# First stage of a hybrid decoder step: transposes, copies and sums in another order

## The chip, the cores and the metric

The kernel runs on one core of one Trainium2 chip. The metric is the device time of one execution in microseconds (us). Engines are called as in the profile: PE is TensorE (PEld its weight loads), DVE is VectorE, ACT is ScalarE, POOL is GpSimd, SP is SyncE, which issues most DMAs.

## What is computed

One decoder layer for a prompt of 1024 tokens and eight single sample tokens, width 1024, all in float32:

```
xn = rmsnorm(h, pre_g)
u, v, z_a, x_b, z_b, g_a, g_b = split(xn @ w_in)          # 1024 -> 7 x 1024
vn = layernorm(gelu(v))
y_a = gelu(u) * chunk_spatial_mix(vn, w_s, b_s) * silu(z_a)
y_b = pool_branch(x_b) * silu(z_b)
m = sigmoid(g_a) * (y_a @ w_pa) + sigmoid(g_b) * (y_b @ w_pb)
h = h + rmsnorm(m @ w_out, post_g)
e = p @ w_ple                                              # p: 256 wide
h = h + rmsnorm(sigmoid(rmsnorm(h, ple_in_g) @ w_pg) * e, ple_out_g)
```

The change touches only what stands at the program's start: the product `e = p @ w_ple`, the first rmsnorm (its squares, roots and scalings of x), and the transposes of x and p.

## The kernel before, in words

Float32 operands are cut in two parts: a high part rounded to TensorE's fp32r by ACT, and a low part, the rest, by DVE (`split`, L352). A product is then three matmuls: high by high, high by low, low by high. The large products use Strassen's seven products on quarters of the operand (`strassen`, L649); the quarters of x are named B11, B12, B21, B22, and sums of them T1 to T4.

All operations are recorded by a planner (L301 is the line that plays them, so nearly every row of the profile names L301; tiles tell them apart). What `begin` (L1743) records is fixed: on each engine it runs in the order in which it is written. What follows is ordered by the planner's costs and due times. Each engine works through its own queue in order, so an instruction that waits holds up all behind it.

`begin` does the following, in the order written:

- DMAs of p (`p_load`), of the two halves of w_ple (`we.fetch`), of x's eight row tiles (`x_load`) and of the first weights (vraw).
- `we.high` and `we.low` (L802, L809) cut w_ple, tile by tile: wehi on ACT, welo on DVE. `p_turn` (L1682) transposes p on PE into a tile pp and cuts it into ph (ACT) and pl (DVE). `embed_terms` (L1700) are the matmuls of e; `embed_out` (L1718) copies a finished e out of PSUM and stores it.
- `norm_root(t)` (L853): ACT squares the row tile t of x and sums it, DVE adds epsilon, POOL raises to the power -0.5. `norm_scale(t)` (L857): DVE scales x's tile in place by that root.
- `x_half(j, kp)` (L872): PE transposes two column blocks (kp) of four row tiles of x (j is 0 for tiles 0 to 3 and 1 for tiles 4 to 7) into a PSUM tile pst, eight 128x128 transposes; ACT and DVE cut pst into high and low. For j = 1 and kp below 2 the cut is left to later sums. `x_out` (L900) copies pst to the buffer `big` (ACT), and `x_whole` (L906) instead writes high plus low of an already cut quarter to `big`, on POOL.
- `x_extra` (L911): eight small transposes of the sample's rows into the tile pxe, which four multiplications by the gain on DVE copy to `big`. `steps[0]` to `steps[3]` are the first Strassen products of v; their `evacuate` copies the accumulator acc out of PSUM on ACT.

PSUM is held in two pools: three regions of two banks, and two single banks. The single banks serve in turn p's pp, w's gain vectors, the first two pst, the accumulators of `steps[0]` to `steps[3]`, pxe and pp again. A tile that takes a bank waits until the tile that held it has been read.

The stretch around the second half of x stands in `begin` as `steps[3].run()`, `x_extra()`, `steps[3].evacuate()`, `p_turn(1, 0)`, `x_half(1, 2)`, `p_turn(1, 1)`, `x_half(1, 3)`, `x_tail()`, `embed(4)`.

Of the kernel before, what the change touches and what calls it, by code (L numbers as in the profile page):

```python
# [13 lines left out]
ALU = mybir.AluOpType  # L14

P = 128
D = 1024
# [4 lines left out]
HALF = 512  # L22
# [285 lines left out]
def hybrid_step(  # L308
# [7 lines left out]
    nc = tc.nc  # L316
# [15 lines left out]
    def slot(name, shape=(P, T), dt=F32):  # L332
        n_name[0] += 1
        return plan.tile(spool.tile(list(shape), dt, tag="slot", name=f"{name}_{n_name[0]}", bufs=SLOTS,
                                    padded_shape=None), "slot")
# [38 lines left out]
    nc = plan  # L374
# [15 lines left out]
    def root(part, n=P, r=None):  # L390

        t, r = sm("ms"), sm("rstd") if r is None else r
        nc.vector.tensor_scalar(out=t[:n], in0=part[:n], scalar1=EPS, scalar2=None, op0=ALU.add)
        nc.gpsimd.tensor_tensor(out=r[:n], in0=t[:n], in1=mhalf[:n], op=ALU.pow)
        return r

    def square_sum(src, n=P, bias=0.0, scratch=None):

        s = sm("ssq")
        out = junk[:n, : src.shape[1]] if scratch is None else scratch[:n]  # L400
        nc.scalar.activation(out=out, in_=src, func=AF.Square, scale=D ** -0.5, bias=bias, accum_out=s[:n])
        return s
# [15 lines left out]
    def quarter(kp, j):  # L418
        both = big[:, 2 * kp : 2 * kp + 2, :].rearrange("p a t -> p (a t)")
        return (both[:, 2 * HALF :] if j else both[:, : 2 * HALF]).rearrange("p (k t) -> p k t", k=2)  # L420
# [431 lines left out]

    def norm_root(t):  # L853
        xt, n = (xe, NS) if t == S else (xts[t], P)
        roots[t] = root(square_sum(xt[:n], n, scratch=slot("squares", (P, D))), n)

    def norm_scale(t):  # L857
        xt, n = (xe, NS) if t == S else (xts[t], P)
# [11 lines left out]
    col = lambda i, k: gvec[:, i * NB + k : i * NB + k + 1]  # L870

    def x_half(j, kp):  # L872

        if kp == 0:
            ps = [bank("pst") for _ in range(2)]
        else:
            ps = region("pst")
            ps = [ps[:, kk] for kk in range(2)]
        for kk in range(2):
            k = 2 * kp + kk  # L880
            for i in range(4):
                nc.tensor.transpose(ps[kk][:, i * P : (i + 1) * P], xts[4 * j + i][:, k * P : (k + 1) * P], ident)
        if j and kp < 2:
            turned[j, kp] = ps
            return
        hi, lo = x_parts(j, kp)
        for kk in range(2):
            nc.scalar.activation(out=hi[:, kk, :HALF], in_=ps[kk], func=AF.Copy, scale=col(0, 2 * kp + kk))
        for kk in range(2):
            nc.vector.scalar_tensor_tensor(out=lo[:, kk, :HALF], in0=ps[kk], scalar=col(0, 2 * kp + kk),  # L890
                                           in1=f32(hi[:, kk, :HALF]), op0=ALU.mult, op1=ALU.subtract)
        turned[j, kp] = ps

    turned = {}

    def x_parts(j, kp):
        what = f"B{kp // 2 + 1}{j + 1}"
        return xop.parts[what, kp % 2] if (what, kp % 2) in xop.parts else xop.new(what, kp % 2)
# [7 lines left out]
    def x_whole(j, kp):  # L906

        hi, lo = (f32(x[:, :, :HALF]) for x in xop.parts[f"B{kp // 2 + 1}{j + 1}", kp % 2])
        nc.gpsimd.tensor_tensor(out=quarter(kp, j)[:, :, :HALF], in0=hi, in1=lo, op=ALU.add)

    def x_extra():  # L911
        ps = bank("pxe").rearrange("p (k t) -> p k t", k=NB)
# [6 lines left out]
    def x_tail():  # L919
        for kp in range(2, NB // 2):  # L920
            split(quarter(kp, 1)[:, :, HALF:], *(x[:, :, HALF:] for x in x_parts(1, kp)))
# [760 lines left out]
    def p_turn(h, q, ks=range(2), by=None):  # L1682
        hi, lo = pcut[h]
        ps = bank("pp").rearrange("p (k c) -> p k c", k=2)
        for k in ks:
            for t in range(2):
                nc.tensor.transpose(ps[:, k, t * P : (t + 1) * P], praw[h][:, 2 * q + t, k * P : (k + 1) * P], ident)
        ks, c = slice(ks[0], ks[-1] + 1), slice(2 * q * P, (2 * q + 2) * P)
        if by is None:
            split(ps[:, ks], hi[:, ks, c], lo[:, ks, c])  # L1690
        else:
            by.tensor_copy(out=hi[:, ks, c], in_=ps[:, ks])
            sub(lo[:, ks, c], ps[:, ks], f32(hi[:, ks, c]))
# [6 lines left out]
    def embed_terms(t, n, terms):  # L1700

        if t == 2:
            e_ps[t, n] = e_ps.get((t, n)) or bank("e")
        elif t not in e_ps:
            e_ps[t] = region("e")
        out = e_ps[t, n] if t == 2 else e_ps[t][:, n]
        todo = left.setdefault((t, n), 6)
        for k, (i, j) in terms:
            nc.tensor.matmul(out, pcut[t // 4][i][:, k, t % 4 * P : (t % 4 + 1) * P], we.at(n, k)[j],
                             start=todo == 6, stop=todo == 1)  # L1710
            todo -= 1
        left[t, n] = todo
# [30 lines left out]
    def begin():  # L1743
        psl = slot("psamp", (P, PLE))
        p_load(0, 0)
        for i, v in enumerate((pre_g, pool_scale, ple_in_g)):
            dma(vecs[i * NB : (i + 1) * NB, :], v[0].rearrange("(k p) -> k p", p=P), nc.scalar)
        we.fetch(0)
        we.fetch(1)
        p_load(0, 1)  # L1750
        for t in range(4):
            x_load(t)
        dma(xe[:NS], x_sample)
        steps[0].loads()
        steps[1].loads()
        for t in range(4, NB):
            x_load(t)
        for q in range(2):
            p_load(1, q)
        dma(psl[:NS], p_sample)  # L1760
        praw.append(psl)
        fetched[0] = 6
        early_loads()

        def busy(n):
            ps = region("warm")[:, 0]
            for _ in range(n):
                nc.tensor.matmul(ps, junk[:, :P], junk, start=True, stop=True)

        p_new(0)  # L1770
        busy(5)
        we.high(0, 0)
        p_turn(0, 0, (0,), nc.vector)
        busy(1)
        p_turn(0, 0, (1,))
        we.high(0, 1)
        for k in range(2):
            we.low(0, k)
        for k in range(2):
            for i in (HH, LH):  # L1780
                for t in range(2):
                    embed_terms(t, 0, [(k, i)])
        for t in range(2):
            embed_terms(t, 0, [(0, HL), (1, HL)])
        for k in range(2):
            we.high(1, k)
        for k in range(2):
            we.low(1, k)
        vps = bank("vecs")
        nc.tensor.transpose(vps[:, : 3 * NB], vecs[: 3 * NB, :], ident[: 3 * NB, : 3 * NB])  # L1790
        nc.vector.tensor_copy(gvec, vps[:, : 3 * NB])
        embed_terms(0, 1, [(0, HH), (0, LH), (1, HH), (1, LH)])
        p_turn(0, 1)
        embed_terms(0, 1, [(0, HL), (1, HL)])
        embed_terms(1, 1, [(0, HH), (0, LH), (1, HH), (1, LH), (0, HL), (1, HL)])
        norm_root(0)
        norm_root(1)
        norm_scale(0)
        embed(2)
        norm_root(2)  # L1800
        embed_out(0, nc.vector)
        norm_root(3)
        norm_scale(1)
        norm_scale(2)
        embed_out(1)
        embed(3)
        norm_scale(3)
        embed_out(2)
        vweights[0].prepare("A11")
        embed_out(3, nc.vector)  # L1810
        for kp in range(3):
            x_half(0, kp)
        vweights[1].prepare("A11")
        x_half(0, 3)
        steps[0].run()
        vweights[0].prepare("A12")
        vweights[1].prepare("A12")
        norm_root(4)
        steps[0].evacuate()
        steps[1].run()  # L1820
        norm_root(S)
        norm_root(5)
        steps[1].evacuate()
        norm_scale(4)
        norm_root(6)
        norm_scale(S)
        norm_root(7)
        for t in range(5, NB):
            norm_scale(t)
        x_whole(0, 0)  # L1830
        x_whole(0, 1)
        steps[2].run()
        steps[2].evacuate()
        x_out(0, 3)
        x_out(0, 2)
        steps[3].run()
        for t in (8, 4, 5):
            steps[t].loads()
        steps[8].loads = None
        x_extra()  # L1840
        steps[3].evacuate()
        p_new(1)
        p_turn(1, 0)
        x_half(1, 2)
        p_turn(1, 1)
        x_half(1, 3)
        x_tail()
        embed(4)
        x_out(1, 2)
        x_half(1, 0)  # L1850
        x_out(1, 0)
        embed_out(4, nc.vector)
        x_out(1, 3)
        x_half(1, 1)
        x_out(1, 1)
        vweights[0].add_up()
        xop.combine("T3")
        embed(5)
        embed_out(5)
        prepared[0] = 4  # L1860
# [52 lines left out]
```

## Time and profile before

| | |
|---|---|
| median of 3 runs | 979.65 us (979.62 to 981.12) |
| the profiled execution's own time | 980.18 us |
| its span, first to last instruction | 978.4 us |
| PE busy | 964.9 us (99%) |
| DVE busy | 799.1 us (82%) |
| ACT busy | 532.3 us (54%) |
| POOL busy | 73.2 us (7%) |
| mean granted PE clock | 0.996 of full speed |

A row of the timeline gives the start, the time it took (merged rows: from the first one's start to the last one's end), engine, line, operation, the tile written and the tiles read with partitions x elements, the count, and in brackets the idle time of the engine before it with what ended it. Rows that follow each other on PE overlap by some 0.15 to 0.25 us, since a matmul's start lies before the end of the one ahead; pace is read from start to start. A row of the windows view gives for each stretch the sum and the time each engine was busy in it, the clock that was granted to PE, the share of the DMA engines and the GB/s.

### The profile page before, as it was taken

The numbers are of one execution on the slowest core, as the hardware profiler recorded it, in microseconds if no ns is written. First come the engines' busy times: TensorE is split into PE (matmuls) and PEld (weight loads), VectorE is DVE, ScalarE is ACT, GpSimd is POOL, SyncE is SP. The second block draws the span as 40 slices with busy tenths as digits, with TensorE's granted clock in tenths as the row PEclk, the third lists the DMA queues.
The fourth block names the chain that finished last, engine by engine and source line by source line (L and its number), as shares of the span: only waits on it lengthen the run. The fifth ranks groups of instructions, "written<-read, shape, count | busy, mean of one in ns | idle before, by whom it ended". The sixth has DMA issues, their size and how long they took to land. (4 is left out here: it accounts for less than half of the span.)

```text
span 978.4 us, 16078 instructions
## 1 busy us (share of the span) xinstructions
PE 964.9 (99%) x6077; PEld 860.4 (88%) x6077; DVE 799.1 (82%) x1263; ACT 532.3 (54%) x899; POOL 73.2 (7%) x143
## 2 busy tenths in 40 slices
PE   9999999999999999999999999999999999999996
PEld 6789999999999999999999999999999986888775
DVE  6796658887789698979897987697799799769786
ACT  6775998865444433344543333552363273967662
POOL 1400000000000000001000100000000001312222
PEclk9999999999999999999999999999999999999999
DMA  9445572422483253656735167884583393799966
GB/s 334 160 151 129 135 171 87 167 94 78 141 298 130 95 187 118 242 196 221 258 131 173 37 228 249 273 312 151 176 302 107 126 349 97 169 280 363 292 183 194
DMA packets 119308, 185.56 MB, mean 190 GB/s; under 512 B 29183, under 2 KB 75735, under 8 KB 119222
## 3 DMA queue, kind: packets, MB, share of 16 engines
q1 hardware_dynamic: 117102, 177.11, 53.8%
q0 software_dynamic: 2080, 7.41, 4.3%
q8 instruction: 48, 0.79, 0.3%
q14 instruction: 30, 0.25, 0.1%
q10 hardware_dynamic: 48, 0.01, 0.0%
HBM read 125.85 MB, written 53.87 MB: 184 GB/s over the span
## 5 line engine op out<-in xcount | busy, mean ns | idle before, releaser
L301 DVE TENSOR_TENSOR u<-acc,u 128x520 f32<-128x520 f32 (+1 forms) x84 | 58.3, 695 | 23.8 <-PE acc L301 21.9
L301 POOL TENSOR_TENSOR rstd<-ms,mhalf 128x1 f32<-128x1 f32 (+1 forms) x36 | 29.7, 825 | 230.1 <-DVE ms L301 208.7
L301 POOL MEMSET u<- 128x8 f32 x32 | 3.3, 104 | 491.3 <-PE acc L301 232.2
L301 ACT ACTIVATE u<-acc 128x512 f32<-128x512 f32 x36 | 21.4, 594 | 23.7 <-PE acc L301 23.1
L301 ACT ACTIVATE paw<-pas 128x512 fp32r<-128x512 f32 x16 | 10.1, 628 | 30.7 <-DVE pas L301 25.5
L301 ACT ACTIVATE pbw<-pbs 128x512 fp32r<-128x512 f32 x16 | 10.0, 629 | 29.3 <-DVE pbs L301 26.1
L301 DVE TENSOR_TENSOR v<-acc,v 128x520 f32<-128x520 f32 (+1 forms) x20 | 13.9, 693 | 12.8 <-PE acc L301 12.6
L301 ACT ACT_TABLE_LOAD x17 | 21.8, 1283 | 4.3 <-PE acc L301 1.8
L301 DVE TENSOR_TENSOR big<-big 128x1024 f32<-128x1024 f32 (+4 forms) x20 | 23.7, 1217 | 0.0
L301 ACT ACTIVATE big<-v 128x1024 uint16<-128x1024 uint16 x16 | 18.6, 1170 | 7.2 <-DMA v<-vw 7.2
L301 PE MATMUL accm<-qh,wpoolw 128*128 128x260 f32 (+1 forms) x96 | 20.9, 320 | 0.0
L301 ACT ACTIVATE zbw<-zbs 128x512 fp32r<-128x512 f32 x16 | 10.0, 628 | 16.5 <-DVE zbs L301 10.2
L301 ACT ACTIVATE gbw<-gbs 128x512 fp32r<-128x512 f32 x16 | 10.0, 624 | 15.7 <-DVE gbs L301 13.7
L301 DVE TENSOR_TENSOR big<-mix,big 128x256 f32<-128x256 f32 x32 | 12.7, 419 | 6.9 <-ACT big L301 6.8
L301 ACT ACTIVATE big<-mix 128x256 f32<-128x256 f32 x32 | 11.7, 379 | 12.4 <-PE mix L301 12.0
L301 DVE TENSOR_TENSOR acc<-acc,u 128x512 f32<-128x512 f32 (+1 forms) x16 | 11.2, 699 | 8.8 <-PE acc L301 8.8
L301 ACT ACTIVATE uw<-us 128x512 fp32r<-128x512 f32 x16 | 10.0, 626 | 14.0 <-DVE us L301 6.8
L301 ACT ACTIVATE vw<-v 128x1024 uint16<-128x1024 uint16 x16 | 16.2, 1045 | 2.3 <-DVE v L301 2.3
L301 PEld LDWEIGHTS accm<-qh,wpoolw 128*128 128x128 f32 x96 | 15.6, 188 | 1.9
L301 ACT ACTIVATE u<-u 128x1032 f32<-128x1032 f32 (+1 forms) x8 | 6.8, 853 | 18.9 <-DVE u L301 18.8
L301 ACT ACTIVATE gb<-gb 128x1032 f32<-128x1032 f32 (+1 forms) x8 | 6.8, 854 | 18.5 <-DVE gb L301 18.5
L301 ACT ACTIVATE zaw<-zas 128x512 fp32r<-128x512 f32 x16 | 10.1, 629 | 12.4 <-PE acc L301 5.2
(666 smaller groups left out, 3599.7 us busy)
## 6 DMA issues: line engine op xcount, KB each, us to landing
ga<-ga SPq DMA_DIRECT2D x16, 516.0 KB
gb<-gb SPq DMA_DIRECT2D x16, 516.0 KB
vraw<-in_w_in_dram SPq DMA_DIRECT2D x22, 256.0 KB
ya<-za SPq DMA_DIRECT2D x8, 516.0 KB
yb<-zb SPq DMA_DIRECT2D x8, 516.0 KB
x<-in_x_prompt_dram SPq DMA_DIRECT2D x8, 512.0 KB
e<-e SPq DMA_DIRECT2D x8, 512.0 KB
garaw<-in_w_in_dram SPq DMA_DIRECT2D x8, 512.0 KB
```

The lines of the kernel that those rows point to most:

```text
L301: getattr(getattr(self.nc, e), method)(*args, **kwargs)
```

## The change

Six edits, all in `begin` and its helpers:

1. `we.low` of w_ple's first tile moves ahead of the second tile's `we.high`, and the matmuls with the first tile's low part ahead of those with the second tile's high part.
2. Among the first row tiles of x, the square of tile 0 moves on ACT ahead of the copy of p's second pp; `embed_out(0)` moves up on DVE, ahead of the scaling of tile 0.
3. The square of x's tile 5 is made by DVE (`square_here`, L404) instead of ACT.
4. The sums `x_whole` are made by DVE instead of POOL, and later: the first after `x_extra`, the second after `x_tail`.
5. `x_half` is split in `x_turn` (transposes) and `x_cut`; for the second half of x, the eight transposes of kp 2 stand ahead of p's first transposes, those of kp 3 ahead of p's second. `steps[3].evacuate()` stands ahead of `x_extra()`.
6. The copy of `embed_out(4)` goes from DVE to ACT and stands ahead of `x_out(1, 0)`.

On PE near the start, one piece of the difference; e_134 and e_135 are e's accumulators of row tiles 0 and 1, wehi_129 and welo_130 hold both tiles of w_ple's first column half, ph and pl are p's parts:

```order
 L301 MATMUL e_134<-wehi_129,pl_127 128x512
 L301 MATMUL e_135<-wehi_129,pl_127 128x512
+L301 MATMUL e_134<-welo_130,ph_126 128x512
+L301 MATMUL e_135<-welo_130,ph_126 128x512
 L301 MATMUL e_134<-wehi_129,ph_126 128x512
 L301 MATMUL e_135<-wehi_129,ph_126 128x512
 L301 MATMUL e_134<-wehi_129,pl_127 128x512
 L301 MATMUL e_135<-wehi_129,pl_127 128x512
-L301 MATMUL e_134<-welo_130,ph_126 128x512 x2
-L301 MATMUL e_135<-welo_130,ph_126 128x512 x2
+L301 MATMUL e_134<-welo_130,ph_126 128x512
+L301 MATMUL e_135<-welo_130,ph_126 128x512
```

Two of the four low-part matmuls now stand ahead of the first matmul that reads the second tile's high part.

On PE after the last product ahead of x's second half, before; p_124 is p's second half, x_89 to x_92 are x's tiles 4 to 7:

```order
L301 MATMUL acc_186<-xB21h_176,vw_180 128x512
L301 MATMUL pxe_207<-ident,xe_84 128x8 x8
L301 MATMUL pp_210<-ident,p_124 128x128 x4
L301 MATMUL pst_211<-ident,x_89 128x128
L301 MATMUL pst_211<-ident,x_90 128x128
L301 MATMUL pst_211<-ident,x_91 128x128
```

and in the change:

```order
L301 MATMUL pxe_207<-ident,xe_84 128x8 x8
L301 MATMUL pst_208<-ident,x_89 128x128
L301 MATMUL pst_208<-ident,x_90 128x128
L301 MATMUL pst_208<-ident,x_91 128x128
L301 MATMUL pst_208<-ident,x_92 128x128
```

These four rows come twice, once for each column block, and pp_211 follows them: p's four transposes have moved behind eight of x's.

On DVE at the same place, before:

```order
L301 TENSOR_SCALAR x_92<-x_92,rstd_203 128x1024
L301 TENSOR_TENSOR big<-pxe_207,gvec 128x2x8 x4
L301 TENSOR_TENSOR pl_209<-pp_210,ph_208 128x2x256
L301 SCALAR_TENSOR_TENSOR xB22l_213<-pst_211,gvec,xB22h_212 128x512 x2
L301 TENSOR_TENSOR pl_209<-pp_214,ph_208 128x2x256
L301 SCALAR_TENSOR_TENSOR xB22l_217<-pst_215,gvec,xB22h_216 128x512 x2
L301 TENSOR_TENSOR xB22l_213<-big,xB22h_212 128x2x8
L301 TENSOR_TENSOR xB22l_217<-big,xB22h_216 128x2x8
L301 COPY e_221<-e_218 128x1024
L301 TENSOR_TENSOR vs_223<-vraw_204 128x512
```

and in the change:

```order
L301 TENSOR_SCALAR x_92<-x_92,rstd_203 128x1024
L301 TENSOR_TENSOR big<-pxe_207,gvec 128x2x8 x4
L301 TENSOR_TENSOR big<-xB11h_166,xB11l_167 128x1024
L301 TENSOR_TENSOR pl_210<-pp_211,ph_209 128x2x256
L301 SCALAR_TENSOR_TENSOR xB22l_213<-pst_208,gvec,xB22h_212 128x512 x2
L301 TENSOR_TENSOR pl_210<-pp_215,ph_209 128x2x256
L301 SCALAR_TENSOR_TENSOR xB22l_217<-pst_214,gvec,xB22h_216 128x512 x2
L301 TENSOR_TENSOR xB22l_213<-big,xB22h_212 128x2x8
L301 TENSOR_TENSOR xB22l_217<-big,xB22h_216 128x2x8
L301 TENSOR_TENSOR big<-xB11h_169,xB11l_170 128x1024
L301 TENSOR_TENSOR vs_223<-vraw_204 128x512
```

The two sums of 128x1024 have come in, one ahead of p's low part and one ahead of the first weight sum vs, and the copy of e has gone to ACT.

The diff:

```diff
@@ norm_root
-        roots[t] = root(square_sum(xt[:n], n, scratch=slot("squares", (P, D))), n)
+        scratch = slot("squares", (P, D))
+        if t in (5,):
+            roots[t] = root(square_here(xt, scratch))
+        else:
+            roots[t] = root(square_sum(xt[:n], n, scratch=scratch), n)
@@ x_half
     def x_half(j, kp):
+        x_turn(j, kp)
+        x_cut(j, kp)
+
+    def x_turn(j, kp):
...
+        turned[j, kp] = ps
+
+    def x_cut(j, kp):
+
         if j and kp < 2:
-            turned[j, kp] = ps
             return
-        hi, lo = x_parts(j, kp)
+        ps, (hi, lo) = turned[j, kp], x_parts(j, kp)
...
@@ x_whole
-        nc.gpsimd.tensor_tensor(out=quarter(kp, j)[:, :, :HALF], in0=hi, in1=lo, op=ALU.add)
+        add(quarter(kp, j)[:, :, :HALF], hi, lo)
@@ begin
         we.high(0, 0)
         p_turn(0, 0, (0,), nc.vector)
+        we.low(0, 0)
         busy(1)
         p_turn(0, 0, (1,))
         we.high(0, 1)
+        we.low(0, 1)
         for k in range(2):
-            we.low(0, k)
-        for k in range(2):
-            for i in (HH, LH):
+            for i in (HH, LH, HL):
                 for t in range(2):
                     embed_terms(t, 0, [(k, i)])
-        for t in range(2):
-            embed_terms(t, 0, [(0, HL), (1, HL)])
...
         embed_terms(0, 1, [(0, HH), (0, LH), (1, HH), (1, LH)])
+        norm_root(0)
         p_turn(0, 1)
         embed_terms(0, 1, [(0, HL), (1, HL)])
+        norm_root(1)
+        embed_out(0, nc.vector)
         embed_terms(1, 1, [(0, HH), (0, LH), (1, HH), (1, LH), (0, HL), (1, HL)])
-        norm_root(0)
-        norm_root(1)
+        norm_root(2)
         norm_scale(0)
         embed(2)
-        norm_root(2)
-        embed_out(0, nc.vector)
...
-        x_whole(0, 0)
-        x_whole(0, 1)
         steps[2].run()
         steps[2].evacuate()
         x_out(0, 3)
         x_out(0, 2)
         steps[3].run()
+        steps[3].evacuate()
         for t in (8, 4, 5):
             steps[t].loads()
         steps[8].loads = None
         x_extra()
-        steps[3].evacuate()
+        x_whole(0, 0)
+        x_turn(1, 2)
         p_new(1)
         p_turn(1, 0)
-        x_half(1, 2)
+        x_cut(1, 2)
+        x_turn(1, 3)
         p_turn(1, 1)
-        x_half(1, 3)
+        x_cut(1, 3)
         x_tail()
+        x_whole(0, 1)
         embed(4)
         x_out(1, 2)
         x_half(1, 0)
+        embed_out(4)
         x_out(1, 0)
-        embed_out(4, nc.vector)
```

More of the change, by code (lines that the diff above doesn't have):

```diff
@@ L891, in x_half @@
                                            in1=f32(hi[:, kk, :HALF]), op0=ALU.mult, op1=ALU.subtract)
-        turned[j, kp] = ps
     turned = {}
```

## The prediction

> **What bounds the kernel now.** I read first the page's busy times, then who TensorE waits for, over the whole span.
>
> ```profile
> PE 964.9 (99%) x6077; PEld 860.4 (88%) x6077; DVE 799.1 (82%) x1263; ACT 532.3 (54%) x899; POOL 73.2 (7%) x143
> ```
> ```profile
> PE pp L301 <- issue: 2.3, 1, 2.3
> PE warm L301 <- DVE junk L301: 1.3, 1, 1.3
> PE e L301 <- ACT wehi L301: 1.0, 1, 1.0
> ```
>
> PE is the bound, and it stops three times in all: once at the start, which the change leaves alone, and twice where it edits. Elsewhere PE works through, so what it gains early is kept unless VectorE or ScalarE then becomes late. Next PE's timeline around the long stop, with DVE and POOL beside it.
>
> ```profile
> 33.32 0.66 PE L301 MATMUL pxe<-ident,xe 8*128 8x8 f32 x8
> 36.30 1.09 PE L301 MATMUL pp<-ident,p 128*128 128x128 f32 x4 [2.32 <-issue]
> 37.17 1.91 PE L301 MATMUL pst<-ident,x 128*128 128x128 f32 x8
> ...
> 40.35 0.48 PE L301 MATMUL e<-wehi,ph 128*128 128x512 f32 x1
> ...
> 43.22 1.91 PE L301 MATMUL pst<-ident,x 128*128 128x128 f32 x16
> 45.11 0.50 PE L301 MATMUL e<-wehi,ph 128*128 128x512 f32 x1
> ```
> ```profile
> 29.05 0.15 DVE L301 TENSOR_SCALAR ms<-ssq 128x1 f32<-128x1 f32 x1 [0.90 <-ACT squares L301]
> ...
> 30.56 0.16 DVE L301 TENSOR_SCALAR ms<-ssq 128x1 f32<-128x1 f32 x1 [0.68 <-ACT squares L301]
> ...
> 31.61 0.15 DVE L301 TENSOR_SCALAR ms<-ssq 128x1 f32<-128x1 f32 x1 [0.22 <-ACT squares L301]
> ...
> 35.79 0.41 DVE L301 TENSOR_TENSOR big<-pxe,gvec 128x16 f32<-128x16 f32 x4
> ```
> ```profile
> 33.18 2.69 DVE L301 TENSOR_SCALAR x<-x,rstd 128x1024 f32<-128x1024 f32 x1
> ```
> ```profile
> 32.82 5.26 POOL L301 TENSOR_TENSOR big<-xB11h,xB11l 128x1024 f32<-128x1024 f32 x2
> ```
>
> The profile names no releaser ("issue"), but pp starts at 36.30, 0.10 after DVE's four multiplications of pxe end (35.79 + 0.41 = 36.20), and in the built program pp lies in pxe's PSUM bank. So PE waited for those four, and they for the last scaling of x ahead of them on DVE, which took 2.69 while POOL made the first of its two sums. The earlier scalings were short:
>
> ```profile
> L301 DVE TENSOR_SCALAR x<-x,rstd 128x1024 f32<-128x1024 f32 x7 | 5.1, 751 | 0.1
> ```
>
> The stop costs more than its length, as the granted clock shows:
>
> ```profile
> 18.40:21.80 3.40, 3.40 (x34) 3.40 (x32) 3.29 (x6) 2.74 (x5) 0.00 (x0) 1.00 1.02 402
> ```
> ```profile
> 35.00:36.00 1.00, 0.00 (x0) 0.00 (x0) 1.00 (x4) 0.00 (x0) 1.00 (x2) 0.98 0.58 143
> 36.00:39.00 3.00, 2.71 (x13) 2.74 (x14) 0.88 (x4) 0.60 (x1) 2.65 (x18) 0.50 0.06 13
> 39.00:40.00 1.00, 1.00 (x10) 1.00 (x8) 0.00 (x0) 0.88 (x2) 0.00 (x0) 0.82 0.00 0
> ```
>
> The third number from the right is the clock. It fell to 0.50 just before 36.0, some 2.0 us after PE's last matmul ended (33.32 + 0.66 = 33.98), and stayed there for about 3.4 us.
>
> **Part 1, w_ple's low part (edit 1).**
>
> ```profile
> 5.62 0.62 PE L301 MATMUL e<-wehi,pl 128*128 128x512 f32 x2
> 7.28 0.73 PE L301 MATMUL e<-wehi,ph 128*128 128x512 f32 x2 [1.03 <-ACT wehi L301]
> ```
> ```profile
> 4.83 0.42 DVE L301 TENSOR_TENSOR pl<-pp,ph 128x256 fp32r<-128x256 f32 x1
> ...
> 5.98 0.69 DVE L301 TENSOR_TENSOR welo<-weraw,wehi 128x512 fp32r<-128x512 f32 x1
> ```
>
> The 1.03 us wait ends with ACT's wehi, which waits for w_ple's second tile from DRAM; that stays. Into it go two low-part matmuls. Their welo can start on DVE at 5.25 (after pl) instead of 5.98 and is there at 5.94, so PE does them from about 6.0 to 6.5, ahead of 7.28. Two matmuls of this width are worth 0.46 (below, the two that start at 25.81 are followed at 26.28). Pushed back on DVE is the low part of p's other block, by 0.7; it is wanted only at 7.5. **-0.46** (0 to -0.46).
>
> The square of x's tile 0 ahead of p's copy on ACT (edit 2) costs nothing if the tile has landed by about 9.4; it had at the latest by 11.67, where its square started without a wait. At that end p's copy comes 1 us later and PE waits 0.4 at `embed(2)`. The scalings come earlier, so that DVE runs ahead of PE by about 0.2 more than before. That matters at one place:
>
> ```profile
> 24.64 1.33 PE L301 MATMUL acc<-xB11h,vw 128*128 128x512 f32 x4
> 25.81 0.63 PE L301 MATMUL acc<-xB11l,vw 128*128 128x512 f32 x2
> 26.28 1.08 PE L301 MATMUL acc<-xB11h,vw 128*128 128x512 f32 x4
> ```
>
> The same four took 1.33 and 1.08: a hidden wait of about 0.25 for vw's low part. I take 0.2 of it. **-0.20** (0 to -0.25). PE then reaches pxe at 33.32 - 0.66 = 32.66.
>
> **Part 2, the long stop (edits 3, 4, 5).** Is DVE ready for x's transposes? DVE's last scaling, clear of POOL, would have ended at 33.18 + 0.75 = 33.93. The square of tile 5 comes in on DVE; priced by the nearest row, also a three-operand instruction of this width, it is 1.28 (and some 0.1 to read its sum):
>
> ```profile
> L301 DVE SCALAR_TENSOR_TENSOR h<-h,rstd,post 128x1024 f32<-128x1024 f32 x8 | 10.2, 1280 | 1.6 <-POOL rstd L301 1.6
> ```
>
> Out go DVE's waits for ACT, 0.90 + 0.68 + 0.22 = 1.80, since ACT makes one square less, and the stretch starts 0.5 earlier: 33.93 + 1.38 - 1.80 - 0.50 = 33.0. PE asks for the last tile at 32.66 + 0.45 (pxe's 0.66 without the overlap of some 0.2 that rows on PE have) + 3 x 0.107 = 33.4. It is ready, by 0.4. The eight transposes then run to 33.97, while DVE's four multiplications (0.41, from about 33.35) end at 33.8. So pp, still in pxe's bank, finds it free. The 24 transposes of x and p take 24 x 0.107 = 2.56 at full clock (the 32 of the stretch 18.40:21.80 took 3.40, at a clock of 1.00). From pxe to e: before 40.35 - 33.32 = 7.03, then 0.45 + 2.56 = 3.01. **-4.02** (-3.1 if DVE is 0.9 later, its two POOL roots slow; -4.2).
>
> **Part 3, what is late next (edits 4 and 6).** After e's twelve matmuls PE comes to the sixteen transposes 43.22 to 45.11; their second half takes the region that ACT empties last, and the e behind them the one that e itself held.
>
> ```profile
> 37.48 0.60 ACT L301 ACTIVATE ph<-pp 128x512 fp32r<-128x512 f32 x1 [2.67 <-PE pp L301]
> 39.12 1.27 ACT L301 ACTIVATE xB22h<-pst,gvec 128x512 fp32r<-128x512 f32 x2 [1.05 <-PE pst L301]
> ...
> 42.11 1.29 ACT L301 ACTIVATE big<-pst,gvec 128x512 f32<-128x512 f32 x2
> ...
> 48.26 1.03 ACT L301 ACTIVATE e<-e 128x1024 f32<-128x1024 f32 x1 [0.82 <-PE e L301]
> ```
>
> ACT's chain from pp: 0.60 + 1.27 + 0.60 + 1.27, two small ones 0.3, and 1.29, less six overlaps of 0.1: 4.8. From pp's landing at 34.6 it ends at 39.4; PE is there at 35.67 + 2.87 + 0.86 = 39.4. The copy of e, now ACT's, ends at 40.4; PE asks for its region at 40.3. I take **+0.3** for both (0 to +0.9). DVE gives up that copy and takes two sums.
>
> ```profile
> 43.83 1.22 DVE L301 COPY e<-e 128x1024 f32<-128x1024 f32 x1
> ```
> ```profile
> L301 DVE TENSOR_TENSOR big<-big x8: 1214/1216/1234, 47.0 to 63.4; 128x1024 f32<-128x1024 f32 x6, 128x1040 f32<-128x1040 f32 x2
> ```
>
> The copy's store waits on SP, ahead of the next weight loads:
>
> ```profile
> 45.08 10.20 SPq L301 DMA_DIRECT2D e<-e  x3
> ```
>
> It could start at 45.08, when DVE's copy was done, and will at 40.4, so nothing behind it is late. The first sum (1.22) lies in DVE's wait for pp's copy, the second takes the copy's place. DVE's weight sums then start some 3.9 earlier than before and PE some 4.4. The tightest place behind is where DVE runs without a break:
>
> ```profile
> 75.22 0.69 DVE L301 TENSOR_TENSOR vw<-vs,vw 128x512 fp32r<-128x512 f32 x1
> ```
> ```profile
> 76.61 0.63 PE L301 MATMUL acc<-xT2h,vw 128*128 128x260 f32 x4
> ```
>
> Ready at 75.91, wanted from 76.6: 0.7 to spare, of which 0.5 is used. Later rows show DVE waiting for PE again.
>
> **Sum.** -0.46 - 0.20 - 4.02 + 0.30 = -4.38. Against the profiled execution (980.18, span 978.4 and 1.78 around it) 975.8; that execution lies 0.53 above the median of the runs, so the median 979.65 becomes 975.3. Own range, all ends together: -2.2 to -4.9, 974.7 to 977.4.
>
> **Rivals.**
> - *DVE is late at the last scaling.* The square and the slow roots on POOL leave PE 1.1 to wait, below the 2.0 after which the clock fell. For it: the spare is 0.4. -3.3: 976.4. Chance 0.14.
> - *Transposes don't keep the clock up.* Then PE goes from the last product's end (33.0) through transposes alone to 35.7, the clock falls after 2.0 and e's matmuls run 3.4 us at half pace, which costs 1.7: -2.7, 977.0. Against it: 18.40:21.80 holds hardly anything but transposes, at 1.00. [...] Chance 0.05.
> - *The change doesn't do what it says.* pp stays in pxe's bank, so the wait is only covered, not gone. If the scaling is long for another reason than POOL's sum, PE stands as long and the clock falls: only part 1 is left, 979.0. For it: one row of 2.69 only. Chance 0.08.
> - *VectorE becomes the bound.* It takes 1.38 + 2.44 - 1.22 = 2.6 more. If its gaps don't take that up, the vw at 75.22 is ready at 78.5 instead of 75.9 and PE, which wants it at 76.6, is 1.9 later than before: 981.5, and 983.2 if the clock falls there too. It decides from 0.7 of lateness against PE's old place. Against it: DVE idles 1.80 before the scalings, and is 1.94 shorter there. Chance 0.06.
>
> **The numbers.** Forecast 0.65, the first two rivals 0.19, the third 0.08, the fourth 0.06; 0.02 for an arrangement that I haven't seen, without a difference. A measurement of this kernel can tell about 0.2% from no change, 2 us: faster means below 977.7. Faster: 0.65 + 0.19 = 0.84 and 0.01 of the third; same: the rest of the third, the unseen and a third of the fourth (981.5 is just under 981.6), 0.11; slower 0.04. The range takes in the forecast's own and the first two rivals, 0.84: 974.5 to 977.5.
>
> **What would show it.** Right: no wait of PE at pp and no clock below 1.00 between 30 and 45; the last scaling of x near 0.75; two low-part matmuls between 6.0 and 6.6; at 60 PE some 4.4 ahead of its old rows. Wrong: a stop of over 1 us at x's or p's transposes (DVE late), a stop of 0.5 or more at the sixteen transposes or the e behind (ACT late), waits at vw between 70 and 80 (VectorE the bound).

## The result, and the profile after

The changed kernel takes **975.80 us** (median of 5 runs, 975.06 to 976.59) against 979.65 (979.61 to 981.12) on the same chip: ratio 0.9958, 95% interval 0.9945 to 0.9972. The forecast was 975.3. The profiled execution took 975.89, 4.29 less than that of before; its span is 973.8 (before 978.4). Busy times, and who PE waits for:

```profile
PE 963.8 (99%) x6077; PEld 858.9 (88%) x6077; DVE 799.4 (82%) x1266; ACT 532.8 (55%) x898; POOL 68.9 (7%) x141
```
```profile
PE warm L301 <- DVE junk L301: 1.3, 1, 1.3
PE acc L301 <- DVE gaw L301: 0.2, 1, 0.2
```

Of the three stops one is left, the one at the start; the 0.2 at gaw is new. PE's timeline at the old long stop, with DVE:

```profile
32.64 0.66 PE L301 MATMUL pxe<-ident,xe 8*128 8x8 f32 x8
33.23 1.09 PE L301 MATMUL pst<-ident,x 128*128 128x128 f32 x8
34.16 0.60 PE L301 MATMUL pp<-ident,p 128*128 128x128 f32 x4
34.60 1.04 PE L301 MATMUL pst<-ident,x 128*128 128x128 f32 x8
35.47 0.60 PE L301 MATMUL pp<-ident,p 128*128 128x128 f32 x4
35.83 0.48 PE L301 MATMUL e<-wehi,ph 128*128 128x512 f32 x1
...
38.70 2.06 PE L301 MATMUL pst<-ident,x 128*128 128x128 f32 x16
40.59 0.50 PE L301 MATMUL e<-wehi,ph 128*128 128x512 f32 x1
```
```profile
27.39 1.20 DVE L301 SCALAR_TENSOR_TENSOR squares<-x 128x1024 f32<-128x1024 f32 x1
...
32.01 0.96 DVE L301 TENSOR_SCALAR x<-x,rstd 128x1024 f32<-128x1024 f32 x1
```
```profile
33.34 0.41 DVE L301 TENSOR_TENSOR big<-pxe,gvec 128x16 f32<-128x16 f32 x4 [0.36 <-PE pxe L301]
33.67 1.22 DVE L301 TENSOR_TENSOR big<-xB11h,xB11l 128x1024 f32<-128x1024 f32 x1
```

The last scaling took 0.96 (forecast 0.75) and ends at 32.97 (forecast 33.0), before PE asks for the tile, and the four multiplications of pxe run under the eight transposes. From pxe to e it is 35.83 - 32.64 = 3.19, before 7.03. The windows view shows the clock (third number from the right) at 1.00 although nothing but transposes ran from 33.2 to 35.8:

```profile
33.00:34.00 1.00, 1.00 (x12) 0.98 (x12) 0.66 (x5) 0.36 (x1) 0.00 (x0) 1.00 0.72 210
34.00:35.00 1.00, 1.00 (x11) 1.00 (x10) 0.89 (x1) 0.14 (x1) 0.00 (x0) 1.00 1.10 300
35.00:36.00 1.00, 1.00 (x11) 1.00 (x10) 0.51 (x1) 1.00 (x3) 0.00 (x0) 1.00 0.85 216
36.00:39.00 3.00, 3.00 (x16) 2.37 (x15) 2.54 (x5) 3.00 (x9) 0.00 (x0) 1.00 0.09 22
```

The start went another way than forecast. PE and ACT there:

```profile
6.33 0.64 PE L301 MATMUL e<-welo,ph 128*128 128x512 f32 x2
6.80 0.62 PE L301 MATMUL e<-wehi,ph 128*128 128x512 f32 x2
...
8.30 0.24 PE L301 MATMUL vecs<-ident,vecs 24*128 24x24 f32 x1
...
17.70 3.55 PE L301 MATMUL pst<-ident,x 128*128 128x128 f32 x31
```
```profile
5.75 0.63 ACT L301 ACTIVATE wehi<-weraw 128x512 fp32r<-128x512 f32 x1
...
10.07 1.06 ACT L301 ACTIVATE squares<-x 128x1024 f32<-128x1024 f32 x1 [1.77 <-DMA x<-in_x_prompt_dram]
...
11.12 0.58 ACT L301 ACTIVATE ph<-pp 128x512 fp32r<-128x512 f32 x1
```

The two low-part matmuls come about where they were expected (6.33 to 6.80, forecast 6.0 to 6.5), but the wait of 1.03 is gone altogether: ACT's second high part began at 5.75 (before 6.60), and PE itself was slower ahead of it, with 0.88 for its first two matmuls of e (4.99 to 5.87), before 0.68 (4.94 to 5.62). Then ACT stood 1.77 for x's first tile with p's copy behind it, and PE lost 0.35: from vecs to the first pst 9.40, before 9.05.

The next table follows five instructions through the executions: each one's start less its start in the first profile of before (the columns give that start). A number that grows between two columns is time lost between them. The kernels are told below.

| kernel | 21.8, first acc | 52.9, end of e | 142.6, acc of gaw | 154.6, mix | 969.4, last matmul |
|---|---|---|---|---|---|
| changed kernel | -0.68 | -4.50 | -4.41 | -3.86 | -4.26 |
| changed_again | -0.87 | -4.68 | -4.56 | -3.23 | -3.64 |
| square_on_scalar | -0.79 | -4.60 | -4.45 | -4.22 | -4.64 |
| p_copy_first | -0.49 | -4.35 | -4.22 | -4.19 | -4.32 |
| both_undone | -0.60 | -4.35 | -4.30 | -3.25 | -3.70 |
| p_first | -0.51 | -3.97 | -3.99 | -3.70 | -3.89 |
| sums_on_pool | -1.30 | -3.90 | -3.95 | -3.62 | -4.03 |
| copy_on_vector | -0.38 | -2.79 | -2.83 | -2.80 | -3.21 |
| sums_on_dve_alone | -0.02 | -2.01 | -2.11 | -2.05 | -2.24 |
| wait_filled | -0.58 | -1.86 | -1.83 | -1.18 | -1.30 |
| front_alone | -0.41 | -1.70 | -1.67 | -0.42 | -0.52 |
| before_again_1 | -0.34 | +0.77 | +0.79 | +0.83 | +0.76 |
| before_again_2 | -0.13 | -1.42 | -1.39 | -1.39 | -1.49 |

Three things are to be seen. The gain arises by 53, and most of it holds to the end. Two profiles of before itself differ by 2.2 at 53. And between 143 and 155 up to 1.3 is lost again, by kernels with the new and with the old order.

### The profile page after: what moved, and what is told of

It is laid out like the page before. It is cut to its first block, busy times and chain, and to the rows that moved or that the text cites. A ratio compares the mean times of both kernels' runs of the same rounds, so it can differ in the third digit from the quotient of the medians.

```text
span 973.8 us, 16071 instructions
## 1 busy us (share of the span) xinstructions
PE 963.8 (99%) x6077; PEld 858.9 (88%) x6077; DVE 799.4 (82%) x1266; ACT 532.8 (55%) x898; POOL 68.9 (7%) x141
## 5 line engine op out<-in xcount | busy, mean ns | idle before, releaser
L301 ACT ACT_TABLE_LOAD x17 | 21.8, 1283 | 4.5 <-PE acc L301 2.0
```

The lines of the kernel that those rows point to most:

```text
L301: getattr(getattr(self.nc, e), method)(*args, **kwargs)
```

## The experiments

The kernels ran in three groups, each on one chip beside the kernel before (medians 979.74, 979.28 and 979.38 there).

**sums_on_pool.** The changed kernel with the two sums back on POOL at their old place:

```diff
-        add(quarter(kp, j)[:, :, :HALF], hi, lo)
+        nc.gpsimd.tensor_tensor(out=quarter(kp, j)[:, :, :HALF], in0=hi, in1=lo, op=ALU.add)
@@ begin: x_whole(0, 0) and x_whole(0, 1) ahead of steps[2].run() again
```

> The changed kernel with edit 4 undone: the two sums of 128x1024 are POOL's again, at their old place. Theory 1 (it was POOL's sum that stretched the last scaling of x): the scaling of x's last tile takes about 2.7 again instead of 0.75 and ends near 34.9; TensorE stops at the fourth of x's transposes for about 1.4, which is below the 2.0 after which the clock fell, so the time is about 977.2; if the clock falls all the same, 978.7. Theory 2 (the new order on TensorE did it, the cover of eight transposes): the scaling may be long or not, TensorE doesn't stop, 975.8.

Measured 977.03 (976.16 to 978.59), ratio to before 0.9973 (0.9964 to 0.9981). DVE's three scalings, POOL, and PE:

```profile
29.75 4.36 DVE L301 TENSOR_SCALAR x<-x,rstd 128x1024 f32<-128x1024 f32 x3
```
```profile
30.88 5.45 POOL L301 TENSOR_TENSOR big<-xB11h,xB11l 128x1024 f32<-128x1024 f32 x2
```
```profile
32.62 0.55 PE L301 MATMUL pst<-ident,x 128*128 128x128 f32 x3
34.16 0.77 PE L301 MATMUL pst<-ident,x 128*128 128x128 f32 x5 [1.00 <-DVE x L301]
```

Beside POOL's sum the three scalings take 4.36, without it 2.45 (sums_on_dve_alone, below). PE waits at the fourth transpose, the one that needs x's last tile, and comes to e 4.40 after pxe, 1.2 later than in the changed kernel. The long scaling is POOL's doing. The stop is 1.0 instead of 2.3, and x's transposes ahead of p's are not the whole reason: the last scaling also ended 2.08 after pxe's start (34.11 - 32.03), in the first profile of before 2.55 (35.87 - 33.32).

**p_first.** The changed kernel with p's transposes ahead of x's, as before:

```diff
-        x_turn(1, 2)
         p_new(1)
         p_turn(1, 0)
-        x_cut(1, 2)
-        x_turn(1, 3)
+        x_half(1, 2)
         p_turn(1, 1)
-        x_cut(1, 3)
+        x_half(1, 3)
```

> The changed kernel with p's transposes ahead of x's again, all else kept. Theory 1: the scaling of x stays short, p's transposes wait only for DVE's four multiplications of the sample's rows, a stop of about 0.5 after the sample's transposes, the clock stays at 1.00: 976.3. Theory 2: a stop of about 2.3 and the clock falls to a half, 979.6.

Measured 975.75 (975.20 to 977.47), ratio 0.9965 (0.9952 to 0.9977). PE:

```profile
32.83 0.66 PE L301 MATMUL pxe<-ident,xe 8*128 8x8 f32 x8
34.04 0.63 PE L301 MATMUL pp<-ident,p 128*128 128x128 f32 x4 [0.56 <-PE pxe L301]
```

pp waits for pxe's bank again, but only 0.56, since the four multiplications are now early; from pxe to e 3.78. Against the changed kernel 0.6 is lost there and 0.2 won back at the sixteen transposes (1.67 instead of 1.89). The cover by x's transposes is worth 0.4 at most, less than the runs can tell.

**sums_on_dve_alone.** The kernel before with the sums on DVE at their new places, and nothing else:

```diff
-        nc.gpsimd.tensor_tensor(out=quarter(kp, j)[:, :, :HALF], in0=hi, in1=lo, op=ALU.add)
+        add(quarter(kp, j)[:, :, :HALF], hi, lo)
@@ begin: x_whole(0, 0) behind x_extra(), x_whole(0, 1) behind x_tail()
```

> The kernel before with edit 4 alone: the two sums on DVE, the first after the sample's four multiplications, the second after the tails of x. Theory 1: the last scaling takes 0.75 and ends at 33.9, p's transposes start at about 34.5 after a stop of 0.5 to 0.6, the clock stays at 1.00, and DVE's copy of e after the second sum makes TensorE wait up to 1.2 at the next e: gain 3.3 less up to 1.2, 976.4 to 977.6. Theory 2 (the cover is what pays): the stop and the clock stay as before, 979.6, or later by the sums, up to 982.

Measured 977.81 (977.23 to 979.82), ratio 0.9983 (0.9974 to 0.9992). PE's waits, and DVE:

```profile
PE e L301 <- ACT big L301: 1.2, 1, 1.2
PE e L301 <- ACT wehi L301: 1.2, 1, 1.2
PE pp L301 <- PE pxe L301: 0.6, 1, 0.6
```
```profile
31.67 2.45 DVE L301 TENSOR_SCALAR x<-x,rstd 128x1024 f32<-128x1024 f32 x3
```

This one edit shortens the stop at pp from 2.3 to 0.6, and the clock doesn't fall (0.997 over the profile): e comes 3.81 after pxe. But 1.2 goes to a new wait at the e behind the sixteen transposes, so that of 3.2 won at e 2.0 is left at 53. Edit 6 takes that wait away (copy_on_vector).

**wait_filled.** The kernel before with ten junk matmuls in the long wait, so that PE is not idle in it:

```diff
         x_extra()
+        busy(10)
```

> The kernel before with ten matmuls of zeros, 0.21 each, in TensorE's long wait, nothing else moved (they compute nothing that is used). Theory 1 (the clock's fall costs by itself): p's transposes start at 36.3 as before, the clock stays at 1.00, the 24 transposes take 2.6 instead of 4.05: 978.1. Theory 2 (the slow transposes come from something else, POOL's sums beside them for instance): the transposes still take 4.0, 979.6.

Measured 978.79 (978.13 to 979.62), ratio 0.9992 (0.9983 to 1.0001). PE:

```profile
33.33 2.33 PE L301 MATMUL warm<-junk 128*128 128x512 bf16 x9
35.73 0.63 PE L301 MATMUL pp<-ident,p 128*128 128x128 f32 x4
36.19 1.04 PE L301 MATMUL pst<-ident,x 128*128 128x128 f32 x8
```

pp still waits for DVE, but the clock stays at 1.00 and from pp to e it is 2.56, in the first profile of before 4.05. So the fall of the clock costs 1.49 by itself in that profile; the medians show 0.95 less, and the interval of their ratio just reaches 1.

**front_alone.** The kernel before with edit 1 alone:

```diff
         p_turn(0, 0, (0,), nc.vector)
+        we.low(0, 0)
...
         we.high(0, 1)
+        we.low(0, 1)
         for k in range(2):
-            we.low(0, k)
-        for k in range(2):
-            for i in (HH, LH):
+            for i in (HH, LH, HL):
```

> The kernel before with w_ple's low part ahead of its second tile, and nothing else. Theory (as predicted): two low-part matmuls fill TensorE's wait for the second tile's high part; the first transposes of x start 0.46 earlier than before (18.38), at about 17.9; the stop at pp and its clock fall stay; time 979.2. Rival: what the changed kernel won at the start (1.03 at vecs) was the earlier landing of w_ple's second tile, not the edit: then ScalarE's second high part starts at 6.6 as before, the wait is as long as before less two matmuls, and where the tile lands at 5.7 the gain is 1.0. In either case under 0.1% of the time, which the times will hardly tell from none; the row of the wait tells it.

Measured 979.52 (978.22 to 980.78), ratio 1.0002 (0.9993 to 1.0011). The first transposes of x start at 17.97, as the theory had it (17.9), but without the edit they start at 18.04 and 18.24 in the further profiles of before and at 17.80 in wait_filled, so this profile doesn't show the edit's worth. ACT's second high part began at 5.62, so the rival's condition wasn't met. What nobody expected is the long stop:

```profile
35.88 0.63 PE L301 MATMUL pp<-ident,p 128*128 128x128 f32 x4 [2.31 <-issue]
36.35 1.04 PE L301 MATMUL pst<-ident,x 128*128 128x128 f32 x8
```

The same stop of 2.31, but the transposes behind it at full pace: this time the clock did not fall (0.998 over the profile). And of the 1.67 that this execution was ahead, 1.25 went between 143 and 155.

**p_copy_first.** The changed kernel with p's copy ahead of x's first square again:

```diff
-        norm_root(0)
         p_turn(0, 1)
+        norm_root(0)
```

> The changed kernel with p's copy ahead of x's first square again on ScalarE. Theory: in the changed kernel ScalarE stood 1.77 us for x's first tile with p's copy behind it, and TensorE waited for the low part of p made from that copy; with the copy first these short waits at embed(2) are gone and the first transposes of x start 0.3 to 0.4 earlier than in the changed kernel (17.70), at 17.3 to 17.4, if the tiles land as they did there; time 975.5. Rival: the wait moves to the scaling of x's first tile, and the transposes of x start at 17.7 or later; time 975.8 to 976.5.

Measured 975.93 (975.75 to 977.33), ratio 0.9967 (0.9954 to 0.9979). From vecs (8.82) to the first pst (17.88) it is 9.06: the 0.34 at `embed(2)` is gone, as the theory said. The start itself came later than its 17.3 to 17.4 (vecs at 8.82 instead of 8.30). The landing of p and w_ple is not the main reason: e's first matmul started only 0.05 later (5.04), but PE was slow for longer (1.00 and 0.81 for the first two pairs of e's matmuls, in the changed kernel 0.88 and 0.46).

**copy_on_vector.** The changed kernel with the copy of e on DVE at its old place:

```diff
-        embed_out(4)
         x_out(1, 0)
+        embed_out(4, nc.vector)
```

> The changed kernel with the copy of e's result back on VectorE, at its place before the change. Theory: VectorE makes the second sum of x first (1.22) and then the copy (1.22), which ends at about 42.4, while TensorE asks for that region at 40.6: a wait of 1.2 to 1.9 at the e behind the sixteen transposes, short enough to leave the clock at 1.00; time 977.0 to 977.7. Rival: the copy's place does not matter, since the sixteen transposes hide it: no wait over 0.3, time 975.8.

Measured 976.81 (976.46 to 977.30), ratio 0.9974 (0.9963 to 0.9984). PE and, beside it, DVE's copy:

```profile
39.01 2.06 PE L301 MATMUL pst<-ident,x 128*128 128x128 f32 x16
42.29 0.50 PE L301 MATMUL e<-wehi,ph 128*128 128x512 f32 x1 [1.22 <-ACT big L301]
```
```profile
41.50 1.22 DVE L301 COPY e<-e 128x1024 f32<-128x1024 f32 x1
```

The wait is there (1.22), the reason is another than the theory's. The copy ends at 42.7, after e has started, so e did not wait for it. It waits for ACT, as the profile says: the next e takes a PSUM region that ACT still empties (its sixth copy to `big` ends at 42.2). With edit 6 it waits for nothing. Whether the copy's engine or its place does that is not shown: edit 6 changes both, and in the kernel before, with the copy on DVE at the same place, the next e waited for DVE's copy and not for ACT (0.17 in before_again_2). The wait of 1.2 in sums_on_dve_alone is listed with the same releaser.

**square_on_scalar.** The changed kernel with tile 5's square back on ACT:

```diff
-        if t in (5,):
+        if t in ():
```

> The changed kernel with tile 5's square back on ScalarE. Theory: with the sum gone from GpSimd the scalings are short whoever makes the square; VectorE saves 1.3 and waits some 1.8 for ScalarE instead, so its last scaling ends at about 33.3 to 33.6 where TensorE asks at 33.4: a wait of 0 to 0.3, time 975.8 to 976.1. Rival: ScalarE's four squares in a row hold the last scaling until 34.5, TensorE waits about 1.0 at x's transposes, time 976.8.

Measured 975.35 (974.95 to 975.87), ratio 0.9959 (0.9946 to 0.9973). DVE's last scaling ends at 33.36 and PE's transposes run on without a wait:

```profile
30.90 2.46 DVE L301 TENSOR_SCALAR x<-x,rstd 128x1024 f32<-128x1024 f32 x3
33.28 0.40 DVE L301 TENSOR_TENSOR big<-pxe,gvec 128x16 f32<-128x16 f32 x4
```

Again 3.19 from pxe to e: edit 3 brings nothing that can be measured.

**both_undone** (the edits of p_copy_first and square_on_scalar together) **and changed_again** (the changed kernel, unedited):

> The changed kernel with two of its edits undone: p's copy ahead of x's first square again, and tile 5's square back on ScalarE. Theory: neither edit carried the gain, and the first one cost 0.34 at embed(2) in the changed kernel's profile; so no wait at embed(2), from vecs to the first transposes of x 9.06 instead of 9.40, no wait at x's transposes, time 975.0 to 975.5, 0.2 to 0.5 under the changed kernel. Rival: ScalarE's later squares hold VectorE, so that the last scaling is late by more than 0.3; time 976 or more.

> The changed kernel itself, beside the variant without two edits and with a second profile. Theory: 975.8; the 3.19 from pxe to e come again within 0.1, the clock stays at 1.00, while the start (pxe at 32.64) and the loss between 140 and 150 (0.5) move with the landing of DMAs by up to 0.6. Rival: the second profile has the same start and the same loss, so they belong to the program and not to DMAs.

Measured 975.48 (975.14 to 976.87) and 975.71 (974.86 to 976.17), ratios to before 0.9964 (0.9950 to 0.9978) and 0.9963 (0.9950 to 0.9975). So no version here beats the changed kernel by more than can be told. In both_undone it is 9.06 from vecs to the first pst and 3.19 from pxe to e without a wait, as its theory said. In changed_again the steps from pxe to e come again (3.18, the clock at 1.00); its start (pxe at 32.47) and its loss between 143 and 155 (1.33 instead of 0.55) do not. Who is late there, DVE and PE in changed_again:

```profile
142.65 0.69 DVE L301 TENSOR_TENSOR gas<-garaw,garaw 128x512 f32<-128x512 f32 x1 [1.22 <-DMA garaw<-in_w_in_dram]
```
```profile
144.84 0.51 PE L301 MATMUL acc<-xT2h,gaw 128*128 128x260 f32 x2 [0.22 <-ACT gaw L301]
...
146.12 0.75 PE L301 MATMUL acc<-xT2h,gaw 128*128 128x260 f32 x4 [0.53 <-DVE gaw L301]
```

DVE waits for a weight tile from DRAM, issued by SP at 134.25: it used it 8.4 later. In p_copy_first the same issue stands at 134.25 too and DVE uses the tile at 141.53, without a wait. front_alone, with the old order, shows 8.2. So there the landing of that transfer decides, and it is not tied to the change. In the changed kernel's first profile DVE stood for another transfer, lnb: it used it at 138.75, 5.83 after its issue (132.92), in the first profile of before 4.95 after (142.55, 137.60).

**before_again_1 and before_again_2**, the kernel before, unedited:

> The kernel before, a second profile. Theory A: a stop of 2.3 at pp always lowers the clock to 0.50 after 2.0, and the 24 transposes behind it take 4.05 from pp's start to e. Theory B: it does so in a part of the executions only, as the start changed alone showed the same stop with the clock at 1.00 and 2.57; then a further profile of before can show 2.57 too.

> The kernel before, a third profile, with the same question: theory A, 4.05 from pp's start to e with the clock at 0.50; theory B, 2.57 with the clock at 1.00 in at least one of these profiles.

The first (980.93), PE and the clock:

```profile
35.95 1.08 PE L301 MATMUL pp<-ident,p 128*128 128x128 f32 x4 [2.32 <-issue]
36.83 1.92 PE L301 MATMUL pst<-ident,x 128*128 128x128 f32 x8
```
```profile
35.00:36.00 1.00, 0.05 (x1) 0.08 (x2) 0.85 (x5) 0.00 (x0) 1.00 (x1) 0.53 0.54 132
...
41.00:42.00 1.00, 1.00 (x5) 0.82 (x4) 1.00 (x2) 0.66 (x2) 0.00 (x0) 0.55 0.00 0
42.00:43.00 1.00, 1.00 (x6) 0.83 (x5) 0.45 (x2) 1.00 (x5) 0.00 (x0) 1.00 0.00 0
```

The second (978.59), PE:

```profile
36.17 0.63 PE L301 MATMUL pp<-ident,p 128*128 128x128 f32 x4 [2.32 <-issue]
36.63 1.04 PE L301 MATMUL pst<-ident,x 128*128 128x128 f32 x8
```

Theory B is right. The stop is 2.32 in all three profiles; behind it the clock is at 0.50 for 3.4, for 6.8 and not at all. From pxe to e it took 7.03, 7.97 and 5.54. The other executions have no trace, but each reports its mean granted clock. Of the 53 executions of before beside these kernels 36 have 0.993 to 0.996, as the two profiles whose clock fell (0.996 and 0.994), and 17 have 0.997 or 0.998, as the third; all eleven of wait_filled have 0.997 or 0.998. By this, an estimate from the means, the clock fell in some two thirds of them.

## Why the prediction was right, and where it was not

**What bounds the kernel.** Right: PE is the bound to the end, and -4.50 at 53 is -4.26 at the last matmul.

**Part 1, edit 1 (-0.46).** Of this size in the mean, not shown by one trace. The wait in the first profile of before was 1.03, in before_again_1 0.9, and in before_again_2 none is listed; it goes by when w_ple's second tile lands (ACT begins on it at 6.60, 6.26 and 5.70) and by when PE comes to its full pace (two matmuls took 0.86 at 6.05 in before_again_2, 0.45 at 7.71). Over the nine profiles with the edit the first product starts 0.67 before that of the first profile of before, over the five without it 0.21: -0.46. Single profiles lie 0.3 or more apart, and eight of the nine hold edit 2 as well, in whole or in part; so that it is just -0.46 is partly luck, and the times of front_alone show no gain.

**Part 1, edit 2 (nothing, or 0.4 at one end).** The step that took the cheap end failed: x's first tile was there between 9.31 and 10.37, in five of six executions after 9.4, and in the two in which it came latest (10.07 in the changed kernel, 10.37 in copy_on_vector) PE lost the 0.34 (p_copy_first shows it gone). **The hidden wait for vw (-0.20)** was not won: the four matmuls take 1.32 in the kernels with the edits too.

**Part 2 (-4.02).** The mechanism was right in each step: POOL's sum made the scaling long (sums_on_pool), the sums' move alone takes the stop from 2.3 to 0.6 (sums_on_dve_alone), the transposes cover the rest. Against the profile that the sum was made on it measured 3.19 - 7.03 = -3.84. What was wrong is to take that profile's clock for the kernel's: over the four profiles with the old stop (7.03, 7.97, 5.54, 5.54) the mean is 6.52, so the part is worth -3.3 in their mean, and in one execution 0 to 2.4 of the saving is the clock. Four profiles are few: in two of them the clock fell, in the 53 executions of before in two thirds. Two things in it were superfluous: the square on DVE (square_on_scalar) and nearly all of the cover (p_first).

**Part 3 (+0.30).** Nothing: the sixteen transposes and the e behind take 40.59 - 38.70 = 1.89, before 45.11 - 43.22 = 1.89. Edit 6 is needed all the same: with the copy left on DVE at its old place, 1.2 is lost there.

**What the sum left out.** The prediction looked for a late engine behind at vw, between 70 and 80, and there was none. The loss came at gaw, between 143 and 155, where DVE waits for lnb or for weights from DRAM: 0.03 to 1.33 in the kernels with the stop shortened, 0 to 1.25 in those with it. Part 2's saving being 0.7 smaller in that mean, and this, are more than the 0.5 between the median, 975.8, and the forecast, 975.3. Against them stands the +0.30 of part 3 that didn't come. So the sum came this near partly by luck: its terms missed in both directions, and the runs themselves spread by 1.5.

**The rivals.** DVE late at the last scaling: not so, it had some 0.5 to spare, and without the spare (sums_on_pool) the price was 1.2. Transposes don't keep the clock up: refuted; in the changed kernel 2.6 of nothing but transposes at 1.00 (33.2 to 35.8). In the first profile of before the clock even came back to 1.00, at 39.4, in a stretch that held transposes alone from 36.3 to 40.3. The change doesn't do what it says: pp does stay in pxe's bank, but finds it free. VectorE becomes the bound: not so.

## What to carry to other kernels

An engine's one long row may be another engine's work (a scaling of 2.69 beside POOL's sum, 0.75 for its like): compare its length with that of its like before pricing what stands behind it. A stop behind which the clock falls in some executions only has no fixed price; the one of 2.3 here cost 1.49 more by the clock in one profile, 2.43 in another and nothing more in two. Take a second profile before its clock enters a sum. And removing a stop pays in full only as far as the next transfer that has no spare, which may lie a hundred microseconds behind: up to 1.33 went again between 143 and 155 here.

## What the runs showed of the hardware

- **The clock.** It fell 2.0 after PE's last matmul in one profile (before, to 0.50 just before 36.0) and 1.4 after it in another (before_again_1, 33.64 to 35.06: a mean of 0.53 in the slice 35 to 36 is 0.06 of it at 1.00 and the rest at 0.50), and not at all in two with the same stop of 2.3 (before_again_2, at 1.00; front_alone, by the pace of its transposes). It stayed low for 3.4 and 6.8. Behind stops of 0.56 (p_first: eight transposes in 1.04) and 1.2 (sums_on_dve_alone: no matmul of e over 0.505) PE went on at full pace, and behind one of 1.00 (sums_on_pool) the windows view shows 1.00. What decides whether a stop of 2.3 lowers the clock is not shown.
- **PE at the start.** Two 128x512 matmuls took 0.86 in before_again_2 (6.05 to 6.91), later 0.45 (7.71 to 8.16). In the changed kernel the first two of e took 0.88 (4.99 to 5.87) and the next two 0.46, though the windows view shows 1.00 for 5 to 6 there. What holds PE up is not shown.
- **DVE beside POOL.** A scaling of 128x1024 took 0.75 (the median of eight in the first profile of before) and 2.69 beside POOL's sum of the same width. The scaling that began at 33.18 ended at 35.87, some 0.4 after POOL's first sum (35.45, an estimate: 32.82 and half of the 5.26 of both sums). Why the sum makes it long is not shown.
- **DMA.** The same transfer landed a microsecond or so apart from one execution to the next: ACT began on w_ple's second tile at 6.60 in the first profile of before, after 0.99 of waiting for it, and at 5.75 in the changed kernel's, without a wait; DVE used the weight tile 8.40 after its issue in changed_again, when it had waited 1.22 for it, and 7.28 after it in p_copy_first, without a wait. That spread is larger than edits 1, 2, 3 and 5 are worth.
